# A hybrid gMLP / DeltaNet / cross-attention layer on one core: the triangular inverses' small matmuls in seven bundles instead of four, the first two projection stages cut by pairs of heads, and a planner with other constants

## The chip, the cores and the metric

The kernel runs on one core of one Trainium2 chip, as one launch. The metric is device time in microseconds (us); lower is better.

## The reference

One decoder layer on 1024 tokens of width 2048, all in float32. Cut to what matters here:

```
h = rmsnorm(x); proj = h @ w_in                       # 2048 x 6672
g_u,g_v,g_z, d_q,d_k,d_v,d_z,d_a,d_b, c_q,c_z = split(proj)
out_a = gelu(g_u) * (tril(W_s) layernorm(gelu(g_v)) + b) * silu(g_z)   # per 128-token chunk
q,k,v = silu(causal_conv4([d_q,d_k,d_v]))             # 8 heads of 128
a = strict_lower((k*beta) k^T * decay)                # per head and chunk of tokens
T = inverse(a + I)                                    # unit triangular
o = scan over chunks with T (gated delta rule)        # state 128 x 128 per head
out_b = rmsnorm(o) * silu(d_z)
out_c = softmax(c_q mk^T / sqrt(128)) mv * silu(c_z)  # 256 memory tokens
x = x + concat(out_a, out_b, out_c) @ w_out; y = rmsnorm(x)
```

The kernel uses chunks of 128 tokens, so an inverse is that of a 128 x 128 unit triangular matrix. There are 64 of them: 8 heads, 8 chunks.

## The kernel before

**The big products.** Each float32 product is done as three fp32r matmuls (high x high, high x low, low x high), so each operand is split: a ScalarE copy makes `hi` (`rhi`, `lh`), a VectorE subtraction makes `lo` (`rlo`, `ll`, `lm`). The two halves of the tokens and two halves of the columns form a 2 x 2 block product, done with seven block products instead of eight (`seven`, in the order 2, 1, 6, 5, 3, 7, 4). A *stage* is one such product of seven. Stages one to three have six output tiles of 128 columns in six PSUM banks (`acc` 0 to 3, `dn` 2 and 3); the later ones have four. Stage one is `project_stage(heads_of(0), ...)` (q, k, v of heads 0 to 3), stage two `heads_of(4)`, stage three `zv`, then `C_U`/`C_Z`, `C_CZ`/`C_CQ`, and the output projection, whose last tile is `kd_515`.

**The weights.** For each pair of row blocks `fetch` loads one rectangle for each entry of `columns` into `raw` (two buffers) or `kept` (four): before, one of 512 and one of 256 columns in stages one to three. All these loads are issued by SP.

**The inverses.** `front` makes the decayed matrices of two heads; `inverse` collects 32 matrices, inverts their 32 x 32 diagonal blocks by substitution on VectorE, writes them to DRAM, and `levels` builds the 64 x 64 and 128 x 128 inverses from them with small matmuls on TensorE: 64 of 32 x 32 (`da = gc t`), 96 of 32 x 32 (three products of each of 16 blocks and two halves), and twice 32 of 64 x 64 (`dy`). There are two such batches, `a` during stage two and `b` during stage three. Results go back to DRAM (`ulo`, `umid`, `uhi`, in the trace `uloa`, `umida`, `uhia` for batch `a`), and `load_u` reads them into `ut` for the scan (`scan_step`), whose first matmul of a batch is `dn<-vs,ut`.

**The order.** Nothing is issued where the code stands. `Plan` records every operation, prices it (`price`), lays all of them out several times with a list scheduler that runs forwards (`lay`) and backwards (`late`), keeps the best layout and issues the operations by their planned times. `R.together()` makes a bundle: its matmuls follow each other on TensorE without anything between. `behind(op)` adds a dependence on `op`. Constants of the planner: `SLACK` is added before TensorE may use another engine's result, `DMA_FIXED` is the assumed latency of a transfer, `PASSES` the number of backward passes. Every engine then runs its instructions in that order, and waits where an operand is not there. As all operations are issued by one line of `issue`, the profile gives L398 for all; groups are told apart by tile names.

Of the kernel before, what the change touches and what calls it, by code (L numbers as in the profile page):

```python
# [17 lines left out]
P = 128  # L18
# [44 lines left out]
class Plan:  # L63
    SEEN = {"pe": 55.0, "act": 35.0, "dve": 35.0, "pool": 78.0, "sp": 60.0}
    SLACK = 300.0
    OVERLAP = {"pe": 0.0, "act": 90.0, "dve": 80.0, "pool": 50.0, "sp": 0.0}
    DMA_RATE = 350.0
    DMA_FIXED = 3800.0
    SWITCH = 400.0
    FIRST, SPREAD, PASSES, STRETCH, AHEAD = 0, 1.75, 5, 1.0, 2000.0  # L70
    TABLE, HOLD = 1300.0, 6000.0
# [111 lines left out]
    def price(self, o, name, outs, ins):  # L183
# [218 lines left out]
def kernel(  # L402
# [629 lines left out]
    def levels(gg, tdr, udr, n):  # L1032
# [19 lines left out]
        with rank(1):  # L1052
# [15 lines left out]
            for h in range(2):  # L1068
                turn_in(uhi[low(2 * h), :, low(0)], every(udr[64:96], h))
            with R.together():  # L1070
                for k in range(16):
                    for r in range(4):
                        t = tu[low(r), k] if r % 2 else tlo[low(r), k, low(0)]
                        PE.matmul(da[low(r), k], gc[low(r), k], t, start=True, stop=True)
            S.copy(yc, da)
            with R.together():
                for k in range(16):
                    for h in range(2):
                        r, q = low(2 * h), low(2 * h + 1)
                        PE.matmul(db[q, k], yc[r, k], tu[r, k], start=True, stop=True)  # L1080
                        PE.matmul(db[r, k], yc[q, k], uhi[q, k, low(1)], start=True, stop=True)
                        PE.matmul(da[q, k], tu[r, k], yc[r, k], start=True, stop=True)
            for h in range(2):
                S.copy(tlo[low(2 * h + 1), :, low(0)], da[low(2 * h + 1)])
                V.tensor_copy(uhi[low(2 * h), :, low(1)], db[low(2 * h)])
            S.copy(ux, db)
            sides = [(x_, h, w) for x_ in range(8) for h in range(2) for w in range(2)]
            with R.together():
                for x_, h, w in sides:
# [198 lines left out]

    def seven(left, right, banks, takes, order, rows=False, last=False, first=0):


        for n, key in enumerate(order):
            c, m = divmod(key, 10)
            bank = banks(key)

            def product(t, i, a, ws, part=None, cols=None):
                for u in range(2):
                    l, (hi, lo) = a[u], ws
                    o = bank[t]
                    if rows:  # L1300
                        l = [x_[:, t * P : (t + 1) * P] for x_ in l]
                        r = [x_[:, u * HT : (u + 1) * HT] for x_ in (hi, lo)]
                        if cols:
                            r, o = [x_[:, cols] for x_ in r], o[:, cols]
# [151 lines left out]

    def rights_of(columns):
        return rights_made([
            (lo, width, lambda i, b, j, k=1, at=at, width=width: blk(w_in, NH * i + j, at[b], k, width))
            for lo, (width, at) in zip((0, 2 * HT), columns)  # L1460
        ])

    def ahead(columns, dst):
# [7 lines left out]

        seven(held_left, [rights_of(columns)], lambda m: wide6, {2: take}, (2,))

    def project_stage(columns, done, dest=None, left=h_left, first_yu=None, then=None, made=None, **how):


        n = len(columns)
        banks, yus, yzs = (wide6, yu6, yz6) if n == 2 else (wide, yu, yz)
        yu2 = first_yu or yus
# [28 lines left out]
        if then:  # L1508
            at = 1
            seven(left, rights, lambda m: banks, takes, ORDER[:1], **how)  # L1510
            how.pop("first")
            then()
        seven(left, rights, lambda m: banks, takes, ORDER[1 if made else at:], **how)
# [137 lines left out]
    Q.dma_start(wt, gmlp_ws[0].rearrange("g t s -> t g s"))  # L1651
    tp = dnr.bufs[1]
# [4 lines left out]
    tp = dnr.bufs[1]  # L1657
    for g in range(NG):
        sl = slice(g * P, (g + 1) * P)
        PE.matmul(tp[:, sl], ones, wsT[g], start=True, stop=True)  # L1660
        V.scalar_tensor_tensor(bt[g], tp[:, sl], col2[:, 4 + g : 5 + g], bsb[:, sl], op0=ALU.mult, op1=ALU.add)
    for hf in range(2):
        spatial(hf)
    scan_banks = dnr.bufs[0:2]
    hand = dnr.bufs[3]
    wide = acc
    el = over([abh[:, 0:HT], ring["tn"].bufs.pop()])
    with rank(2.6):
        for hf in range(2):
            for n in range(2):  # L1670
# [104 lines left out]

    def total(r):
        V.scalar_tensor_tensor(r[:, 4:5], r[:, 3:4], 1.0 / D, r[:, 4:5], op0=ALU.mult, op1=ALU.add)

    def close(half_, t):

        r, r0 = ssy[half_][t], half_ * HT + t * P
        total(r)
        rsqrt_to(r[:, 5:6], r[:, 4:5])
# [13 lines left out]

    def square(half_, t, c, cols=slice(0, HT)):
        S.activation(jk[:, cols], ys[half_][t][c][:, cols], AF.Square, accum_out=ssy[half_][t][:, c : c + 1])

# [29 lines left out]
    def out_pair(cp):  # L1830
# [14 lines left out]
        def final(m, key, c, after=None):  # L1845
            put = more(m, key, after)

            def take(t, a, cols=slice(0, HT)):
                r = ssy[key[0]][t]
                if cols.stop - cols.start < HT:  # L1850
                    add(y[key][t][:, cols], a[:, cols], y[key][t][:, cols])
                    square(key[0], t, c, cols)
                    total(r) if cols.start == 0 else close(key[0], t)
                    return
                put(t, a)
                square(key[0], t, c)
                if c == 3:
                    close(key[0], t)
# [60 lines left out]
```

## Time and profile before

| what | value |
|---|---|
| median of 3 runs | 1586.66 us (1584.83 to 1587.31) |
| profiled execution | 1587.73 us |
| its span, first to last instruction | 1586.0 us |
| mean granted TensorE clock | 0.995 |
| busy: PE / PEld / DVE / ACT / POOL | 98% / 83% / 77% / 59% / 6% |
| DMA | 431.40 MB, mean 272 GB/s |

The profile page names the engines PE (TensorE matmul), PEld (its weight loads, beside PE), DVE (VectorE), ACT (ScalarE), POOL (GpSimd) and SP (SyncE, which here issues nearly all DMAs; SPq is its sequencer). Busy time is the union of an engine's instructions; a matmul is shown with its latency, so neighbours overlap, and the time that one costs is the distance to the next start. "Idle before" is an engine's idle time ahead of a group, with what ended it. PEclk is the share of full clock that TensorE was granted.

### The profile page before, as it was taken

The numbers are of one execution on the slowest core, as the hardware profiler recorded it, in microseconds if no ns is written. First come the engines' busy times: TensorE is split into PE (matmuls) and PEld (weight loads), VectorE is DVE, ScalarE is ACT, GpSimd is POOL, SyncE is SP. The second block draws the span as 40 slices with busy tenths as digits, with TensorE's granted clock in tenths as the row PEclk, the third lists the DMA queues.
The fourth block names the chain that finished last, engine by engine and source line by source line (L and its number), as shares of the span: only waits on it lengthen the run. The fifth ranks groups of instructions, "written<-read, shape, count | busy, mean of one in ns | idle before, by whom it ended". The sixth has DMA issues, their size and how long they took to land.

```text
span 1586.0 us, 25201 instructions
## 1 busy us (share of the span) xinstructions
PE 1559.0 (98%) x8773; PEld 1309.6 (83%) x8773; DVE 1219.6 (77%) x1802; ACT 931.7 (59%) x1921; POOL 102.1 (6%) x125
## 2 busy tenths in 40 slices
PE   8999999999999999999999999999999999999997
PEld 7987888888888778888888778888888888888886
DVE  6966844789979756887799667878668888688775
ACT  7832455767854247778864444876657864344455
POOL 0100001010020001110110010000000000000001
PEclk9999999999999999999999999999999999999999
DMA  9999866999988797886989896898868979678657
GB/s 328 305 333 330 288 182 201 323 324 336 301 260 275 236 294 245 263 282 193 276 275 319 240 261 218 279 343 284 257 211 267 310 263 351 214 269 294 227 151 274
DMA packets 338353, 431.40 MB, mean 272 GB/s; under 512 B 77353, under 2 KB 163890, under 8 KB 338226
## 3 DMA queue, kind: packets, MB, share of 16 engines
q1 hardware_dynamic: 336642, 427.09, 84.0%
q0 software_dynamic: 1088, 2.10, 0.4%
q8 instruction: 69, 1.13, 0.3%
q10 hardware_dynamic: 496, 0.61, 0.1%
q14 instruction: 58, 0.48, 0.1%
HBM read 330.29 MB, written 99.42 MB: 271 GB/s over the span
## 4 chain that ended last, share of the span: by engine, by line
PE 85%; DMA 4%; issue 1%; ACT 1%; DVE 1%; SPq 1%; POOLq 0%; POOL 0%; ACTq 0%; DVEq 0%
PE acc L398 53%; PE dn L398 32%; SPq L398 1%; DMA raw<-in_w_in_dram 1%; DMA E<-ed 1%; DMA late<-os 0%; DMA xr<-pd 0%; DMA kd<-late 0%; DMA ut<-uloa 0%; DMA ut<-in_x_dram 0%; DMA qT<-late 0%; DMA ll<-hsd 0%; ACT obs L398 0%; DVE tn L398 0%; ACT rhi L398 0%
## 5 line engine op out<-in xcount | busy, mean ns | idle before, releaser
L398 PE MATMUL acc<-lh,rhi 128*128 128x512 f32 x1024 | 396.6, 396 | 1.8 <-DVE obs L398 1.8
L398 PE MATMUL acc<-lh,rlo 128*128 128x512 f32 x1024 | 387.1, 396 | 0.2 <-DVE rlo L398 0.2
L398 ACT CAST rhi<-raw 128x1024 fp32r<-128x1024 f32 (+1 forms) x148 | 186.6, 1261 | 244.8 <-PE dn L398 119.3
L398 DVE TENSOR_TENSOR rlo<-raw,rhi 128x1024 fp32r<-128x1024 f32 (+1 forms) x148 | 219.3, 1482 | 106.6 <-ACT rhi L398 103.1
L398 PE MATMUL acc<-ll,rhi 128*128 128x512 f32 x688 | 269.9, 397 | 0.0
L398 PEld LDWEIGHTS acc<-lh,rhi 128*128 128x128 f32 x1024 | 193.3, 189 | 39.4 <-DVE obs L398 2.6
L398 PEld LDWEIGHTS acc<-lh,rlo 128*128 128x128 f32 x1024 | 193.0, 189 | 37.5 <-DVE rlo L398 0.7
L398 DVE TENSOR_TENSOR ll<-ll,lh 128x1024 fp32r<-128x1024 f32 x122 | 149.9, 1229 | 17.3 <-ACT lh L398 17.0
L398 PEld LDWEIGHTS acc<-ll,rhi 128*128 128x128 f32 x688 | 129.7, 189 | 24.8 <-DVE ll L398 0.2
L398 ACT CAST lh<-ll 128x1024 fp32r<-128x1024 f32 x122 | 127.9, 1048 | 23.2 <-DMA ll<-hsd 5.6
L398 PE MATMUL acc<-lm,rhi 128*128 128x512 f32 x336 | 133.4, 399 | 0.0
L398 PE MATMUL dn<-lh,rhi 128*128 128x512 f32 x288 | 112.9, 393 | 0.4 <-issue 0.4
L398 PE MATMUL dn<-lh,rlo 128*128 128x512 f32 x288 | 107.6, 393 | 0.0
L398 DVE TENSOR_TENSOR raw<-raw,kept 128x1024 f32<-128x1024 f32 (+1 forms) x56 | 81.1, 1452 | 3.6 <-DMA raw<-in_w_in_dram 3.6
L398 PE MATMUL dn<-ll,rhi 128*128 128x512 f32 x192 | 75.4, 394 | 0.0
L398 PEld LDWEIGHTS acc<-lm,rhi 128*128 128x128 f32 x336 | 63.6, 189 | 12.0
L398 DVE TENSOR_TENSOR rlo<-kept,rhi 128x1024 fp32r<-128x1024 f32 (+1 forms) x29 | 41.9, 1446 | 37.2 <-ACT rhi L398 37.1
L398 ACT CAST rhi<-kept 128x1024 fp32r<-128x1024 f32 (+1 forms) x29 | 35.7, 1230 | 51.4 <-PE dn L398 25.6
L398 POOL TENSOR_TENSOR hs<-hs,mhalf 128x4 f32<-128x4 f32 x32 | 45.8, 1436 | 273.7 <-DVE hs L398 262.6
L398 PEld LDWEIGHTS dn<-lh,rhi 128*128 128x128 f32 x288 | 54.3, 188 | 10.8
L398 PEld LDWEIGHTS dn<-lh,rlo 128*128 128x128 f32 x288 | 53.9, 188 | 10.4
L398 POOL TENSOR_TENSOR small<-small,mhalf 128x1 f32<-128x1 f32 x26 | 21.3, 819 | 580.7 <-DVE small L398 580.7
(412 smaller groups left out, 3395.8 us busy)
## 6 DMA issues: line engine op xcount, KB each, us to landing
raw<-in_w_in_dram SPq DMA_DIRECT2D x120, 512.0 KB
ll<-hsd SPq DMA_DIRECT2D x54, 512.0 KB
raw<-in_w_out_dram SPq DMA_DIRECT2D x48, 512.0 KB
raw<-in_w_in_dram SPq DMA_DIRECT2D x72, 256.0 KB
lm<-hsd SPq DMA_DIRECT2D x26, 512.0 KB
pd<-obs SPq DMA_DIRECT2D x48, 256.0 KB
late<-os SPq DMA_DIRECT2D x44, 256.0 KB
kept<-in_w_in_dram SPq DMA_DIRECT2D x20, 512.0 KB
```

What stands on the lines that cost most here:

```text
L398: o.fn(*o.args, **o.kw)
```

## The change

- `levels`: the first bundle of 64 becomes two of 32, each with its own copy of half the result (`yc`, 128 x 256 instead of 128 x 512). The bundle of 96 becomes three of 32, one product each, the second and third `behind` the one before. The 64 x 64 bundles stay at 32; the first of them is also `behind` the bundle before it. So 4 bundles become 7 in each of the two batches, with the same matmuls.
- `Plan`: `SLACK` 300 to 200, `DMA_FIXED` 3800 to 4200, `PASSES` 5 to 7, and a new `FETCH` of 3500 added to the latency of small matmuls.
- Stages one and two: `heads_of` gives three rectangles of 256 columns (q, k and v of a pair of heads) instead of one of 512 and one of 256; `lay_of` gives each output tile's place in the buffer. The first column half now holds q, k, v of heads 0 and 1 (or 4 and 5).
- The spatial gate's transposes use PSUM bank `dn` 2 instead of `dn` 1, and its two halves are issued each just ahead of that half's scans.
- The last output tile is finished in one piece of 512 columns instead of two of 256.

```diff
@@ class Plan
-    SLACK = 300.0
+    SLACK = 200.0
-    DMA_FIXED = 3800.0
+    DMA_FIXED = 4200.0
-    FIRST, SPREAD, PASSES, STRETCH, AHEAD = 0, 1.75, 5, 1.0, 2000.0
+    FIRST, SPREAD, PASSES, STRETCH, AHEAD = 0, 1.75, 7, 1.0, 2000.0
+    FETCH = 3500.0
@@ price
-            o.lat = 175.0
+            o.lat = 175.0 + (0.0 if out.shape[0] == P or n == P or name == "transpose" else self.FETCH)
@@ levels
+            for e in range(2):
+                ks = slice(8 * e, 8 * e + 8)
+                with behind(R.ops[-1] if e else R.gate), R.together():
+                    for k in range(16)[ks]:
+                        for r in range(4):
+                            t = tu[low(r), k] if r % 2 else tlo[low(r), k, low(0)]
+                            PE.matmul(da[low(r), k], gc[low(r), k], t, start=True, stop=True)
+                S.copy(yc[:, ks], da[:, ks])
+            blocks = [(k, h, low(2 * h), low(2 * h + 1)) for k in range(16) for h in range(2)]
             with R.together():
-                for k in range(16):
-                    for r in range(4):
-                        t = tu[low(r), k] if r % 2 else tlo[low(r), k, low(0)]
-                        PE.matmul(da[low(r), k], gc[low(r), k], t, start=True, stop=True)
-            S.copy(yc, da)
-            with R.together():
-                for k in range(16):
-                    for h in range(2):
-                        r, q = low(2 * h), low(2 * h + 1)
-                        PE.matmul(db[q, k], yc[r, k], tu[r, k], start=True, stop=True)
-                        PE.matmul(db[r, k], yc[q, k], uhi[q, k, low(1)], start=True, stop=True)
-                        PE.matmul(da[q, k], tu[r, k], yc[r, k], start=True, stop=True)
+                for k, h, r, q in blocks:
+                    PE.matmul(da[q, k], tu[r, k], yc[r, k], start=True, stop=True)
             for h in range(2):
                 S.copy(tlo[low(2 * h + 1), :, low(0)], da[low(2 * h + 1)])
+            with behind(R.ops[-1]), R.together():
+                for k, h, r, q in blocks:
+                    PE.matmul(db[r, k], yc[q, k], uhi[q, k, low(1)], start=True, stop=True)
+            for h in range(2):
                 V.tensor_copy(uhi[low(2 * h), :, low(1)], db[low(2 * h)])
+            with behind(R.ops[-1]), R.together():
+                for k, h, r, q in blocks:
+                    PE.matmul(db[q, k], yc[r, k], tu[r, k], start=True, stop=True)
             S.copy(ux, db)
-            with R.together():
+            with behind(R.ops[-1]), R.together():
                 for x_, h, w in sides:
...
@@ seven
-                        at = u * HT + t * P if t < NT else 2 * HT + u * HT // 2 + t % NT * P
+                        at = lay[t][0] + u * lay[t][1]
-                    if last and key == order[-1] and t == NT - 1:
-                        for cols in (slice(0, HT // 2), slice(HT // 2, HT)):
-                            for h in held:
-                                product(t, *h, cols=cols)
-                            takes[key](t, bank[t], cols)
-                        return
@@ project_stage and around
+    def lay_of(columns):
+        los = [sum(2 * w for w, _ in columns[:i]) for i in range(len(columns))]
+        return [(lo + c, w) for lo, (w, _) in zip(los, columns) for c in range(0, w, P)]
-            which, h = (b, h0 + t) if t < NJ else (2, h0 + 2 * b + t - NJ)
+            which, h = t // 2, h0 + 2 * b + t % 2
-        return (HT, (C_Q + c, C_K + c)), (half, (C_DV + c, C_DV + c + half))
+        return tuple((half, (c0 + c, c0 + c + half)) for c0 in (C_Q, C_K, C_DV))
@@ spatial gate
-            bank = dnr.bufs[1]
+            bank = dnr.bufs[2]
-    for hf in range(2):
-        spatial(hf)
-    with rank(2.6):
-        for hf in range(2):
+    for hf in range(2):
+        spatial(hf)
+        with rank(2.6):
             for n in range(2):
                 back_of(2 + n, hf, inv)
```

Three places show what the planner makes of it. The first is TensorE in batch `a`, where the kernel before goes from the bundle of 64 to that of 96. `dn_111` and `dn_112` are the banks of the small products, `gt_434`, `gt_435`, `inv_432`, `inv_433` their operands (`inv_433` holds `yc`); rows on `acc` are matmuls of the running stage.

```order
L398 MATMUL dn_111<-gt_434,inv_432 32x32
L398 MATMUL dn_111<-inv_432 32x32
L398 MATMUL acc_110<-lh,rhi_76 128x512
L398 MATMUL acc_107<-lh,rhi_77 128x512
L398 MATMUL acc_107<-ll,rhi_77 128x512
L398 MATMUL acc_107<-lh,rlo_75 128x512
L398 MATMUL dn_112<-inv_432,inv_433 32x32
L398 MATMUL dn_112<-gt_435,inv_433 32x32
L398 MATMUL dn_111<-inv_433,inv_432 32x32
```

The changed kernel at its third bundle of the same batch:

```order
L399 MATMUL acc_109<-ll,rhi_77 128x512
L399 MATMUL acc_110<-lh,rhi_77 128x512
L399 MATMUL acc_110<-ll,rhi_77 128x512
L399 MATMUL acc_109<-lh,rlo_75 128x512
L399 MATMUL acc_109<-lh,rhi_77 128x512
L399 MATMUL dn_111<-inv_433,inv_432 32x32 x32
L399 MATMUL acc_109<-ll,rhi_77 128x512
L399 MATMUL acc_109<-lh,rlo_75 128x512
L399 MATMUL acc_110<-lh,rlo_75 128x512
L399 MATMUL acc_110<-lh,rhi_77 128x512
```

Before, four matmuls of the stage stand between 64 and 96 small ones; now 18 stand ahead of this bundle of 32 and 19 behind it. Over both batches the gaps are 18 to 25 matmuls; before they were 4, 8 and 4.

The second place is ScalarE in batch `a`. `inv_433<-dn` is the copy of `yc`, `gt_434<-dn` the next copy that batch needs; CAST rows split the stage's operands. Before:

```order
L398 CAST rhi_77<-raw_73 128x1536
L398 CAST lh<-ll 128x1024
L398 COPY inv_433<-dn_111 128x512
L398 COPY inv_433<-dn_112 128x512
L398 COPY gt_434<-dn_111 32x16x32 x2
L398 COPY inv_432<-dn_111 128x512
```

Now:

```order
L399 CAST rhi_77<-raw_73 128x1536
L399 COPY inv_433<-dn_111 128x256
L399 CAST rhi_76<-raw_72 128x1536
L399 COPY inv_433<-dn_111 128x256
L399 CAST lh<-lm 128x1024
L399 COPY gt_434<-dn_111 32x16x32 x2
```

The second half of `yc` now stands behind the cast of a freshly loaded weight tile, `raw_72`.

The third place is SP's queue between batch `a` and the first scan step, which reads `ut_82`. Before:

```order
L398 DMA umida<-gt_434 64x16x64 x2
L398 DMA ut_82<-uloa 32x8x32
L398 DMA ll<-h0d 128x2x512
L398 DMA kept_80<-in_w_in_dram 128x2x512
L398 DMA ut_82<-uhia 64x8x64
L398 DMA kept_80<-in_w_in_dram 128x2x256
L398 DMA raw_72<-in_w_in_dram 128x2x512
L398 DMA ut_82<-umida 64x8x64
```

Now:

```order
L399 DMA ut_82<-uloa 32x8x32
L399 DMA ll<-h0d 128x2x512
L399 DMA ut_83<-uloa 32x8x32
L399 DMA raw_73<-in_w_in_dram 128x2x512
L399 DMA raw_73<-in_w_in_dram 128x2x256
L399 DMA umida<-gt_434 64x16x64 x2
L399 DMA ll<-h0d 128x2x512
L399 DMA ut_82<-umida 64x8x64
```

The last load that the scan step needs, `ut_82<-umida`, now follows its store with one load between instead of six.

More of the change, by code (lines that the diff above doesn't have):

```diff
@@ L1085, in levels @@
+            for h in range(2):
                 V.tensor_copy(uhi[low(2 * h), :, low(1)], db[low(2 * h)])
+            sides = [(x_, h, w) for x_ in range(8) for h in range(2) for w in range(2)]
+            with behind(R.ops[-1]), R.together():
+                for k, h, r, q in blocks:
+                    PE.matmul(db[q, k], yc[r, k], tu[r, k], start=True, stop=True)
             S.copy(ux, db)
-            sides = [(x_, h, w) for x_ in range(8) for h in range(2) for w in range(2)]
-            with R.together():
+            with behind(R.ops[-1]), R.together():
@@ L1287, with seven @@
     ends, chunk_ends = {}, [kvmark[-1]] * 8
-    def seven(left, right, banks, takes, order, rows=False, last=False, first=0):
+    def seven(left, right, banks, takes, order, lay=None, rows=False, last=False, first=0):
         for n, key in enumerate(order):
@@ L1294, in seven, with product @@
             bank = banks(key)
-            def product(t, i, a, ws, part=None, cols=None):
+            def product(t, i, a, ws, part=None):
                 for u in range(2):
@@ L1457, in rights_of @@
     def rights_of(columns):
+        los = [sum(2 * w for w, _ in columns[:i]) for i in range(len(columns))]
         return rights_made([
             (lo, width, lambda i, b, j, k=1, at=at, width=width: blk(w_in, NH * i + j, at[b], k, width))
-            for lo, (width, at) in zip((0, 2 * HT), columns)
+            for lo, (width, at) in zip(los, columns)
         ])
+    def lay_of(columns):
+        los = [sum(2 * w for w, _ in columns[:i]) for i in range(len(columns))]
+        return [(lo + c, w) for lo, (w, _) in zip(los, columns) for c in range(0, w, P)]
     def ahead(columns, dst):
@@ L1470, in take @@
                 Q.dma_start(dst[t], o)
-        seven(held_left, [rights_of(columns)], lambda m: wide6, {2: take}, (2,))
+        seven(held_left, [rights_of(columns)], lambda m: wide6, {2: take}, (2,), lay_of(columns))
     def project_stage(columns, done, dest=None, left=h_left, first_yu=None, then=None, made=None, **how):
         n = len(columns)
-        banks, yus, yzs = (wide6, yu6, yz6) if n == 2 else (wide, yu, yz)
+        lay = lay_of(columns)
+        banks, yus, yzs = (wide6, yu6, yz6) if n > 1 else (wide, yu, yz)
         yu2 = first_yu or yus
@@ L1509, in project_stage @@
             at = 1
-            seven(left, rights, lambda m: banks, takes, ORDER[:1], **how)
+            seven(left, rights, lambda m: banks, takes, ORDER[:1], lay, **how)
             how.pop("first")
             then()
-        seven(left, rights, lambda m: banks, takes, ORDER[1 if made else at:], **how)
+        seven(left, rights, lambda m: banks, takes, ORDER[1 if made else at:], lay, **how)
     def to_heads(h0):
         def done(hf, b, t, y):
-            which, h = (b, h0 + t) if t < NJ else (2, h0 + 2 * b + t - NJ)
+            which, h = t // 2, h0 + 2 * b + t % 2
             Q.dma_start(p_d[which][h][:, hf * HT : (hf + 1) * HT], y)
@@ L1651 @@
     Q.dma_start(wt, gmlp_ws[0].rearrange("g t s -> t g s"))
-    tp = dnr.bufs[1]
+    tp = dnr.bufs[2]
     for g in range(NG):
@@ L1656 @@
         V.tensor_tensor(out=wsT[g], in0=tp[:, g * P : (g + 1) * P], in1=utri, op=ALU.mult)
-    tp = dnr.bufs[1]
+    tp = dnr.bufs[2]
     for g in range(NG):
@@ L1774 @@
     ys = [[[None] * 4 for _ in range(NT)] for _ in range(2)]
-    def total(r):
-        V.scalar_tensor_tensor(r[:, 4:5], r[:, 3:4], 1.0 / D, r[:, 4:5], op0=ALU.mult, op1=ALU.add)
     def close(half_, t):
         r, r0 = ssy[half_][t], half_ * HT + t * P
-        total(r)
+        V.scalar_tensor_tensor(r[:, 4:5], r[:, 3:4], 1.0 / D, r[:, 4:5], op0=ALU.mult, op1=ALU.add)
         rsqrt_to(r[:, 5:6], r[:, 4:5])
@@ L1796, in close, with square @@
             to.dma_start(out[r0 : r0 + P, c * HT : (c + 1) * HT], y)
-    def square(half_, t, c, cols=slice(0, HT)):
-        S.activation(jk[:, cols], ys[half_][t][c][:, cols], AF.Square, accum_out=ssy[half_][t][:, c : c + 1])
+    def square(half_, t, c):
+        S.activation(jk, ys[half_][t][c], AF.Square, accum_out=ssy[half_][t][:, c : c + 1])
     oh = halves(own(os, "oh", "alo1", 4 * HT))
@@ L1846, in final, with take @@
             put = more(m, key, after)
[L1848 to L1854, printed above, removed]
+            def take(t, a):
                 put(t, a)
                 square(key[0], t, c)
+                r = ssy[key[0]][t]
                 if c == 3:
```

2 lines of the change are left out of this document (removed).

## The prediction

> **What bounds the kernel now.** I read the page's first lines, then TensorE's waits, then fine windows around the places with waits, then the chain.
>
> ```profile
> PE 1559.0 (98%) x8773; PEld 1309.6 (83%) x8773; DVE 1219.6 (77%) x1802; ACT 931.7 (59%) x1921; POOL 102.1 (6%) x125
> ...
> q8 instruction: 69, 1.13, 0.3%
> ```
>
> TensorE is busy for 1559.0 of 1586.0 us. No rearrangement takes its matmuls away, so the change can only win what TensorE loses: 27 us of idle time at most, and slow stretches that count as busy. Its waits, with times and the longest:
>
> ```profile
> PE dn L398 <- issue: 5.8, 5, 2.4
> ...
> PE dn L398 <- DMA ut<-uloa: 2.7, 1, 2.7
> PE acc L398 <- DVE obs L398: 1.8, 1, 1.8
> PE dn L398 <- DVE tn L398: 1.7, 1, 1.7
> ...
> PE dn L398 <- DVE kd L398: 0.7, 1, 0.7
> ```
>
> The largest entry waits for nothing that the profile shows. The windows put it at the inverses' bundles (first batch near 552 us, second near 901 us); the first row is a steady stretch for comparison:
>
> ```profile
> core 0: us, PE busy (x), PEclk, DMA share, GB/s
> 280.00:320.00 40.00, 40.00 (x180) 1.00 0.97 326
> 552.77:556.18 3.41, 2.32 (x193) 1.00 0.95 332
> 556.18:559.60 3.42, 3.42 (x10) 0.50 1.06 344
> 576.67:580.08 3.41, 1.19 (x6) 1.00 1.14 279
> 580.08:583.49 3.41, 2.93 (x9) 0.50 1.17 262
> 900.93:904.34 3.41, 1.58 (x121) 1.00 0.92 283
> 904.34:907.75 3.41, 3.41 (x8) 0.50 0.88 259
> ```
>
> Three windows with idle time (1.1, 2.2 and 1.8 us idle of 3.41) are each followed by one of 3.41 us at half clock. A half-clock window does half its work, so it costs 3.41 x 0.5 = 1.7 us, though the second column shows it as busy.
>
> Why would TensorE starve in its own small matmuls? The queue q8 moved 1.13 MB in 69 packets, 16.4 KB each, and 8773 matmuls plus as many weight loads are 17546 instructions, 64 B each: q8 has the size of TensorE's code, fetched in blocks of about 256 instructions. A steady stretch uses 180 x 2 instructions in 40 us, 9 per us; the window at 552.77 uses 193 x 2 in 2.32 busy us, 166 per us. So a bundle of 96 runs through a block in under 2 us. That the stalls are fetches is inferred, not shown.
>
> **The change part by part.** All sums are against the profiled execution, 1587.73 us (span 1586.0 and 1.73 around it), which is 1.07 above the median of 1586.66; the forecast is moved to the median at the end.
>
> *Seven bundles, spread out.* The price of a small matmul and of a switch, from TensorE's timeline at the first bundle of 64, and of an ordinary matmul, from the chain:
>
> ```profile
> 549.80 0.39 PE L398 MATMUL acc<-ll,rhi 128*128 128x512 f32 x1
> 550.02 0.39 PE L398 MATMUL acc<-lh,rlo 128*128 128x512 f32 x1
> 550.34 0.21 PE L398 MATMUL dn<-gt,inv 32*32 32x32 f32 x1
> ...
> 551.44 0.19 PE L398 MATMUL dn<-inv 32*32 32x32 f32 x1
> 551.56 0.73 PE L398 MATMUL acc<-lh,rhi 128*128 128x512 f32 x2
> ...
> 1337.37 65.28 PE acc L398 x288
> ```
>
> An ordinary matmul takes 65.28 / 288 = 0.227 us. From the last one before the bundle to the first behind it are 1.54 us, so 64 small ones cost 1.31: 0.09 to enter, 1.10 for the run, 0.12 to leave. A bundle of 32 then costs about 0.75, and each extra bundle adds 0.2: six of them, +1.2 us (0.6 to 1.8). Against that, 32 small and 18 ordinary matmuls are now 100 instructions in 0.75 + 18 x 0.227 = 4.8 us, 21 per us, an eighth of the density that stalled. I take all 5.8 us of "issue" as gone, and with them the half-clock windows at 556 and 904 us, 2 x 1.7 = 3.4. The Trainium skill, Runtime: NRT & Kernel Launch, section "Instruction fetch mechanics", says that instructions come in blocks of 16 KiB and that the cost of crossing one is mostly hidden. The packet size agrees; a hidden cost would leave the 5.8 us unexplained, and by that rule this term would be nothing (a rival below).
>
> *The copies between bundles.* TensorE runs in order, so a bundle whose operand is late holds up the whole stage. In the first batch the second half of `yc` stands on ScalarE behind the cast of `raw_72`, which waits for a weight load:
>
> ```profile
> L398 ACT CAST rhi<-raw 128x1536 fp32r<-128x1536 f32 x72 | 106.8, 1483 | 131.1 <-PE dn L398 95.4 <-DVE raw L398 8.5 <-DMA sm<-od 8.4
> L398 ACT ACT_TABLE_LOAD x19 | 24.4, 1283 | 2.8 <-issue 2.2 <-DVE small L398 0.3
> L398 ACT COPY inv<-dn 128x512 f32<-128x512 f32 x8 | 4.7, 587 | 21.4 <-PE dn L398 11.9 <-DVE gt L398 4.7 <-issue 4.7
> ...
> 551.96 1.87 SPq L398 DMA_DIRECT2D raw<-in_w_in_dram  x2
> ...
> 119.00 5.78 DMA ut<-in_x_dram
> ...
> 916.38 10.58 DMA raw<-in_w_in_dram
> ```
>
> TensorE reaches its third bundle 2 x 0.75 + 36 x 0.227 = 9.7 us after the first. If SP issues `raw_72` where it does now, 1.6 to 3.5 us after the first bundle (551.96 against 550.34, two issues), a landing takes 5.8 us as in the row at 119, the cast 1.5 and the half copy at most 0.6, the copy is ready 11.4 us after it: a wait of about 2 us. An idle time of 2.2 us brought a half-clock window at 580 us, so this one is at the edge of it; I leave it out. With the 10.58 us of the row at 916 it is 6.5, plus 1.7. I take +2.0 (0 to 8.2). ScalarE also gets 16 more table loads (35 for 19 in the order), 16 x 1.28 = 20.5 us; it is idle for 41% of the span, so nothing, except where one stands ahead of such a copy: 1.3.
>
> *The first scan step.* The wait for `ut` (2.7 us, and the half-clock window at 580) hangs on SP's queue:
>
> ```profile
> 567.68 1.30 SPq L398 DMA_DIRECT2D umida<-gt  x2
> ...
> 573.18 0.61 SPq L398 DMA_DIRECT2D ut<-umida  x1
> ```
>
> Store and load now stand closer (one load between, not six), but the store itself has 19 issues ahead of it since the last bundle. At the 0.65 us that one of the two stores takes, 19 + 4 issues are 15 us, with two landings behind; TensorE gets there 76 matmul times, 17 us, after the last bundle. It will be late again. I take no change (from -4.4, both gone, to +3).
>
> *Spatial gate's bank and order of the second scans.* TensorE's work there is the same and hidden in the stage; the wait for `obs` at a stage's start (1.8) had a weight load of 10.58 us behind it that shares the queues with batch `b`. I take half of it as gone, -0.9 (-1.8 to 0).
>
> *Column blocks by pairs.* 56 more loads on SP, with rows of 1 KB for 2 KB:
>
> ```profile
> 555.88 2.46 SPq L398 DMA_DIRECT2D kept<-in_w_in_dram  x3
> ...
> SPq L398 <- PE dn L398: 222.8, 129, 7.8
> ```
>
> 56 x 0.82 = 46 us of SP's time, which lies in the 222.8 us that SP waits for TensorE alone. Where SP is the limit, in the start (TensorE's wait for `tn`, 1.7 us, ends a chain through SP and the load of `x` at 119), seven of them stand ahead of the last `x` load: at most 7 x 0.82 = +5.7, at best -1.7, as that load is the 130th on SP now and was the 132nd. I take 0. That conv and `qk` of the first pair could start earlier moves VectorE's and ScalarE's work, not TensorE's.
>
> *The last tile.* Two halves cost a wait, the 0.7 us for `kd`:
>
> ```profile
> 1573.84 0.28 PE L398 MATMUL dn<-oh 128*128 128x256 f32 x1
> ...
> 1577.59 0.28 PE L398 MATMUL dn<-rhi,fl 128*128 128x256 f32 x1
> ...
> 1574.04 0.69 DVE L398 TENSOR_TENSOR kd<-dn,kd 128x512 f32<-128x512 f32 x1 [0.72 <-PE dn L398]
> ...
> 1577.91 0.42 DVE L398 TENSOR_TENSOR kd<-dn,kd 128x256 f32<-128x256 f32 x1
> ...
> 1574.83 0.63 ACT L398 ACTIVATE jk<-kd 128x512 bf16<-128x512 f32 x1
> ...
> 1578.72 0.42 ACT L398 ACTIVATE jk<-kd 128x256 bf16<-128x256 f32 x1 [0.53 <-DVE kd L398]
> ```
>
> Whole, 12 matmuls of 0.227 from 1573.84 start last at 1576.34, 1.25 earlier than 1577.59, and last 0.1 longer; the final add and square are 0.27 and 0.21 longer. Net -0.7 at best; as the add now stands behind the scaling of the tile before, I take -0.5 (-0.7 to +0.6).
>
> *Less slack for TensorE.* Results may be planned 0.1 us closer to their use. All its waits outside the places above are under 3 us, so I take +1.0 (0 to 3).
>
> Sum: -5.8 - 3.4 + 1.2 + 2.0 - 0.9 - 0.5 + 1.0 = -6.4 us. That is 1587.73 - 6.4 = 1581.3 for a profiled execution, 1580.3 on the scale of the median.
>
> **The rivals.**
>
> *Late operands at the bundles (slower).* Each batch now hands over between TensorE and a copy six times where it did three, at fixed places in the stage. If in both batches one copy waits behind a cast whose weight load takes 10.58 us, each costs 6.5 + 1.7 = 8.2: -6.4 - 2.0 + 16.4 = +8, 1594.7. It is a loss from 11.6 us of such waits on. For it: ScalarE's order above, a DMA share of 0.9 to 1.1 in those windows, less slack. Against: TensorE has 4 us of other work between bundles and waited for no copy at all in the kernel before. Chance 0.18.
>
> *The stalls are not fetches (it doesn't do what it says).* Small matmuls then starve for another reason, in 14 bundles as in 8, and the half-clock windows stay too. The sum is +1.2 + 2.0 - 0.9 - 0.5 + 1.0 = +2.8, 1589.5. For it: the profile names no releaser. Against: the density. Chance 0.06. The rule of the Trainium skill quoted above would give this case.
>
> *SP pays at the start.* With +5.7 there, the sum is -0.7: 1586.0. For it: the chain through SP at 119. Against: the `x` load moved ahead by two places. Chance 0.10.
>
> *The scan's wait goes too.* -6.4 - 4.4 = -10.8, 1575.9; with the other good ends -17, 1569.5. It belongs to the faster side.
>
> **How the numbers follow.** What a measurement can tell from no change is 0.2%, 3.2 us: below 1583.5 is faster, above 1589.8 slower. The forecast with its better cases has 0.66, and nearly all of that lies below 1583.5. The start's rival and half of the fetch rival end within 0.2%, with 0.02 of the forecast's own upper end: 0.15 in all. The late copies and what is left make 0.19. The range reaches from 1571 (short of the sum of all best ends) to 1590 (the fetch rival inside, the slower one outside).
>
> **What would show it.** Right: no "issue" entry above 1 us in TensorE's waits; PEclk 1.00 at 550 to 570 and 895 to 925; the entry `ut<-uloa` or its neighbour still there with 1 to 5 us; a last matmul some 1.2 us earlier against the end of the tile before it. Wrong: "issue" at the bundles, which would refute the density; or new entries for ACT `inv` or `gt`, or DMA `raw`, of more than 2 us there, which is the slower rival; or `tn` above 4 us in the first 160 us.

## The result, and the profile after

| | before | after |
|---|---|---|
| median | 1586.93 us (1584.83 to 1587.31, 4 runs) | 1575.95 us (1574.93 to 1577.73, 4 runs) |
| ratio to before | | 0.9934, 95% interval 0.9919 to 0.9949 |
| profiled execution | 1587.73 us, span 1586.0 | 1575.38 us, span 1573.7 |
| mean granted clock | 0.995 | 0.999 |

The change is faster by 11.0 us, inside the range; the forecast was 6.4. Half of this document is about what those 11 us are made of, because the last runs showed that they are not all owed to the change.

The page's lines for the kernel after: the busy times and the packets.

```profile
PE 1556.9 (99%) x8761; PEld 1307.3 (83%) x8761; DVE 1220.2 (78%) x1800; ACT 954.9 (61%) x1937; POOL 98.2 (6%) x125
...
DMA packets 353585, 431.40 MB, mean 274 GB/s; under 512 B 78249, under 2 KB 193458, under 8 KB 353458
```

TensorE is busy for 2 us less, though more bundles lengthen its work; the half-clock windows of the kernel before count as busy time. The pair blocks bring 15,000 more packets (338,353 before) for the same bytes. TensorE's waits of the kernel after, complete (total, times, longest):

```profile
PE dn L399 <- DMA y<-in_mem_norm_g_dram: 3.0, 1, 3.0
PE dn L399 <- ACT inv L399: 1.6, 1, 1.6
PE dn L399 <- DMA kept<-in_mem_dram: 1.2, 1, 1.2
PE dn L399 <- ACT rhi L399: 1.0, 1, 1.0
PE dn L399 <- ACT vs L399: 0.5, 2, 0.2
PE acc L399 <- ACT xr L399: 0.3, 1, 0.3
PE dn L399 <- DVE states L399: 0.2, 1, 0.2
```

"Issue" (5.8), `ut` (2.7), `obs` (1.8), `tn` (1.7) and `kd` (0.7) are gone; the entries for `y`, `kept` and `rhi` belong to the first 10 us and are as before. One new entry is large, 1.6 us for `inv`, the copy between two bundles; the other small ones (`vs`, `xr`, `states`) come to 1.0 us, where the kernel before had 0.8 (`os`, `rlo`, `vs`). Three stretches of both kernels, TensorE alone (width, busy, matmul records, clock, DMA share, GB/s): the end of stage one, batch `a`, batch `b`. Before:

```profile
340.00:500.00 160.00, 160.00 (x778) 1.00 0.93 301
500.00:620.00 120.00, 115.57 (x959) 0.97 0.85 256
880.00:960.00 80.00, 73.91 (x748) 0.98 0.84 235
```

After:

```profile
340.00:500.00 160.00, 160.00 (x776) 1.00 0.95 304
500.00:620.00 120.00, 118.16 (x965) 1.00 0.77 238
880.00:960.00 80.00, 80.00 (x791) 1.00 0.89 246
```

Width less busy is the idle time: 4.4 + 6.1 = 10.5 us at the two batches before, 1.8 after, and no half-clock window after. These three rows are the yardstick for the experiments.

### The profile page after: what moved, and what is told of

Same layout as the page of the kernel before. It is cut to its first block, busy times and chain, and to the rows that moved or that the text cites. A ratio compares the mean times of both kernels' runs of the same rounds, so it can differ in the third digit from the quotient of the medians.

```text
span 1573.7 us, 25225 instructions
## 1 busy us (share of the span) xinstructions
PE 1556.9 (99%) x8761; PEld 1307.3 (83%) x8761; DVE 1220.2 (78%) x1800; ACT 954.9 (61%) x1937; POOL 98.2 (6%) x125
## 4 chain that ended last, share of the span: by engine, by line
PE 96%; DVE 1%; issue 1%; DMA 1%; ACT 0%; SPq 0%; POOLq 0%; POOL 0%; ACTq 0%
PE acc L399 59%; PE dn L399 37%; DMA raw<-in_w_in_dram 0%; DMA kept<-in_mem_dram 0%; DVE os L399 0%; DVE states L399 0%; DVE rlo L399 0%; ACT vs L399 0%; DVE obs L399 0%; DVE raw L399 0%; ACT jk L399 0%; DVE ll L399 0%; DVE steps L399 0%; SPq L399 0%; ACT obs L399 0%
## 5 line engine op out<-in xcount | busy, mean ns | idle before, releaser
L399 PE MATMUL acc<-lh,rhi 128*128 128x512 f32 x1024 | 389.7, 395 | 0.0
L399 PE MATMUL acc<-lh,rlo 128*128 128x512 f32 x1024 | 380.0, 394 | 0.1
L399 POOL TENSOR_TENSOR small<-small,mhalf 128x1 f32<-128x1 f32 x26 | 16.3, 630 | 681.7 <-DVE small L399 681.7
L399 DVE TENSOR_TENSOR lm<-lm,lh 128x1024 fp32r<-128x1024 f32 x42 | 51.2, 1219 | 7.4 <-ACT lh L399 7.3
L399 PE MATMUL acc<-rlo,lh 128*128 128x512 f32 x144 | 56.3, 391 | 0.0
```

Of the source, the lines that this page charges most:

```text
L399: o.fn(*o.args, **o.kw)
```

## The experiments

Twelve kernels ran. Ratios are to the kernel before on the same chip. The last three columns come from rows like those above: idle time in 500 to 620 and 880 to 960 us together, half-clock windows of 3.41 us in there, idle time in 340 to 500 us. They come from one profiled execution each, and executions of one kernel scatter: the kernel before, run 27 times beside e1 to e4, lay between 1581.3 and 1592.1 us, so differences of an us or two between rows mean little.

| kernel | blocks | bundles | constants | median us | ratio, 95% | idle at batches | half clock | idle 340–500 |
|---|---|---|---|---|---|---|---|---|
| before | old | 4 | old | 1586.93 | 1 | 10.5 | 3 | 0 |
| e1 | old | 7 | old | 1585.16 | 0.9983 (0.9969–0.9997) | 4.4 | 2 | 0 |
| e7 | pairs | 4 | old | 1592.16 | 1.0019 (1.0008–1.0031) | 12.3 | 5 | 0 |
| e2 | old | 4 | new | 1587.31 | 1.0006 (0.9995–1.0016) | 6.1 | 1 | 1.1 |
| e11 | pairs | 7 | new, `FETCH` 0 | 1595.43 | 1.0059 (1.0046–1.0071) | 5.1 | 4 | 0 |
| **after** | pairs | 7 | new | 1575.95 | 0.9934 (0.9919–0.9949) | 1.8 | 0 | 0 |
| e6 | pairs | 4 | new | 1576.82 | 0.9922 (0.9910–0.9934) | 3.3 | 0 | 0 |
| e10 | pairs | 7 | new, `DMA_FIXED` 4300 | 1581.48 | 0.9970 (0.9959–0.9980) | 0.6 | 0 | 1.1 |
| e5 | old | 7 | new | 1586.81 | 0.9998 (0.9986–1.0010) | 3.2 | 0 | 3.5 |
| e9 | pairs | 7 | new, `SLACK` 210 | 1588.00 | 1.0008 (0.9999–1.0016) | 0.8 | 0 | 3.2 |
| e12 | pairs, old bank | 7 | new | 1588.01 | 1.0014 (1.0005–1.0023) | 3.0 | 0 | 4.4 |
| e3 | old | 7 | new | 1591.34 | 1.0038 (1.0024–1.0051) | 2.6 | 0 | 7.4 |

e1, e2, e3 and e7 are the kernel before with parts of the change; e5, e6, e9 to e12 the changed kernel with parts undone.

**What starves the bundles: e4 and e8.** Both add 192 matmuls of 32 x 32, on constants that are always there, to stage one of the kernel before; nobody reads their results. e4 has them in one block, e8 in six bundles with 36 stage matmuls between. The edit (e4, the matmul's operands shortened; in e8 `22 <= len(chunk_ends) < 28` and `range(32)`):

```diff
                     chunk_ends.append(R.ops[-1])
+                    if len(chunk_ends) == 22:
+                        with rank(-1), behind(R.ops[-1]), R.together():
+                            for z in range(192):
+                                zr = slice(z % 4 * 32, z % 4 * 32 + 32)
+                                PE.matmul(dnr.bufs[1][zr, ...], ident[zr, zr], ident[zr, zr], ...)
```

> The kernel before with 192 additional 32x32 matmuls on resident constants in one block in stage one, near 240 us, far from the batches; they wait for nothing and nobody reads them. Theory (instruction fetch): 384 instructions in about 3.3 us, so an 'issue' wait of 1 to 4 us in or just behind the block, and a half-clock window after it; 4 to 9 us more in all. Rival (the stalls at the batches were waits on operands that the profile does not name): no 'issue' wait there, 3.3 us more.

> The kernel before with the same 192 additional 32x32 matmuls as in the dense block, in six bundles of 32 with 36 stage matmuls between them. Theory (instruction fetch): no 'issue' wait and PEclk 1.00 from 190 to 245 us; about 6 x 0.75 = 4.5 us more there. Rival (small matmuls starve TensorE wherever they stand): waits and half-clock windows near each bundle, 8 us or more.

One execution each: 1600.90 us for e4, 1595.22 for e8 (the kernel before on the same chip, in the median: 1586.11 and 1588.18). e4, TensorE's waits between 195 and 225 us, and then its windows at the block:

```profile
PE dn L398 <- issue: 7.8, 2, 4.5
```

```profile
200.24:203.66 3.42, 1.97 (x195) 1.00 0.91 277
203.66:207.07 3.41, 0.40 (x46) 1.00 0.77 210
207.07:210.48 3.41, 1.35 (x104) 0.50 0.34 112
210.48:213.90 3.42, 2.13 (x66) 0.50 0.02 5
213.90:217.31 3.41, 3.41 (x10) 0.50 0.63 172
```

e8, the stretch that holds all six bundles:

```profile
190.00:250.00 60.00, 60.00 (x628) 1.00 0.63 175
```

The same matmuls stall for 7.8 us in one block and for nothing in six. No operand can be late there, so it is their density. (The second stall lies in windows with a DMA share of 0.34 and 0.02, so it is not a crowd on the queues either; the first lies at 0.91 and 0.77.) What was expected of e8 came true in this stretch; of e4 the kind came true and the size was too small: 7.8 us of stalls for 1 to 4, three half-clock windows for one, and 14.8 us in all for 4 to 9. Both also stall longer than the kernel before at the old bundles of the two batches, 8.6 us in e4 and 11.3 in e8 where it has 5.8. So the length of these stalls is no fixed price of a bundle.

The records say more. The stretch from one "issue" stall to the next, in the kernel before at batch `b`, in e4 at its block and in e8 at batch `a`:

```profile
902.74:908.94 6.20, 5.05 (x128) 0.72 0.85 267
908.94:913.00 4.06, 3.36 (x127) 1.00 0.65 189
```

```profile
206.66:211.76 5.10, 1.75 (x128) 0.54 0.30 99
```

```profile
568.49:574.41 5.92, 2.50 (x128) 0.50 1.07 364
```

These neighbouring stalls (twelve such pairs in seven kernels) are 127 or 128 matmul records apart, with as many weight loads some 256 instructions. That is the block of the prediction, 16.4 KB or one packet of q8 at 64 B an instruction: TensorE stops each time where a block of its code ends. The traces also hold every packet of q8, 16,384 bytes each, with its times. Beside TensorE's stalls (us from the span's start):

| kernel | q8 packet, from and to | TensorE goes on at | after a stall of | packet's end to going on |
|---|---|---|---|---|
| before | 900.32 to 901.29 | 902.76 | 2.40 | 1.47 |
| before | 906.59 to 907.57 | 908.95 | 1.15 | 1.38 |
| e4 | 203.86 to 205.23 | 206.67 | 4.46 | 1.44 |
| e4 | 209.38 to 210.33 | 211.77 | 3.35 | 1.44 |
| e8 | 572.08 to 573.09 | 574.42 | 3.42 | 1.33 |

The kernels together have 31 stalls called "issue". 28 of them end 1.1 to 1.5 us after a packet of q8 has landed, though these packets come only every 23 us in the mean. So these stalls are code fetches, which the prediction could only infer. The other three (e1 0.5 us, e2 1.4, e8 0.2) stand ahead of the first scan step's `dn<-vs,ut`, 5 to 13 us after the last such packet; what they wait for is not shown. The Trainium skill, Runtime: NRT & Kernel Launch, section "Instruction fetch mechanics", has the same block of 256 instructions and calls the crossing mostly hidden: that holds in e8's stretch (nothing at six bundles) and fails at e4's block (4.5 and 3.3 us at two crossings).

**One part at a time: e1, e2, e7.** e1 is the kernel before with the change's `levels`:

```diff
+            for e in range(2):
+                ks = slice(8 * e, 8 * e + 8)
+                with behind(R.ops[-1] if e else R.gate), R.together():
...
+            with behind(R.ops[-1]), R.together():
+                for k, h, r, q in blocks:
```

> The kernel before with the seven smaller bundles alone; the planner keeps its old constants, so the bundles stand 3 to 7 stage matmuls apart (in the changed kernel 18 to 25). Theory (TensorE starves for instructions where small matmuls stand densely): the density hardly falls, so 'issue' waits of 4 to 7 us and at least two half-clock windows remain; 1584 to 1590 us. Rival (the size of a bundle is what counts): 'issue' under 1 us, 1577 to 1580 us.

Its bundles stand 3 to 7 stage matmuls apart, as nothing tells the planner to spread them. "Issue" falls from 5.8 to 2.2 us (1.7 of it fetches), less than the 4 to 7 that were expected, and two half-clock windows stay:

```profile
PE dn L398 <- issue: 2.2, 3, 1.1
...
PE dn L398 <- ACT inv L398: 1.5, 1, 1.5
```

e2 is the kernel before with the four constants, and so with distance but with the old bundles:

```diff
-    SLACK = 300.0
+    SLACK = 200.0
-    DMA_FIXED = 3800.0
+    DMA_FIXED = 4200.0
-    FIRST, SPREAD, PASSES, STRETCH, AHEAD = 0, 1.75, 5, 1.0, 2000.0
+    FIRST, SPREAD, PASSES, STRETCH, AHEAD = 0, 1.75, 7, 1.0, 2000.0
+    FETCH = 3500.0
```

> The kernel before with the planner's new constants alone (SLACK, DMA_FIXED, PASSES, FETCH); four bundles of 64, 96, 32 and 32, now 19 to 28 stage matmuls apart. Theory (density): the bundle of 96 still runs through 192 instructions in under 2 us, so 0 to 2 us of 'issue' per batch, and the rest of the stalls goes; 1577 to 1583 us. Rival (bundle size): 'issue' stays at 4 to 6 us, 1584 us or more.

```profile
PE acc L399 <- issue: 3.6, 1, 3.6
...
PE dn L399 <- issue: 1.8, 2, 1.4
```

Still 5.4 us of it (4.0 of it fetches), and no gain, as the rival had it. e7 is the kernel before with the pair blocks:

```diff
-        return (HT, (C_Q + c, C_K + c)), (half, (C_DV + c, C_DV + c + half))
+        return tuple((half, (c0 + c, c0 + c + half)) for c0 in (C_Q, C_K, C_DV))
```

> The kernel before with the column blocks by pairs alone: old bundles, constants, spatial gate and last tile. Theory (TensorE had no waits in stage one before, so earlier fronts give nothing): 'issue' stays at 4 to 7 us, 1584 to 1589 us. Rival (the blocks bring a gain of their own): 1576 to 1582 us.

It is slower than either expectation, with 8.6 us of "issue". So no part alone was measured to give more than 0.2%.

**Two parts, or the change less one: e3, e5, e6.** e3 has e1's and e2's edits together; e5 is the changed kernel with the old blocks (e7's edit turned round); e6 is the changed kernel with the four old bundles.

> The kernel before with bundles and constants together, and nothing of the column blocks, the spatial gate's bank or the last tile. Theory (the gain is the batches' stalls, half-clock windows and the wait for ut, and all of it comes from these two edits): no 'issue' entry, PEclk 1.00 at both batches, 1575 to 1579 us. Rival (the pairs of heads bring a large part): 1581 to 1585 us.

> The changed kernel with the old column blocks (512 and 256) in stages one and two. Theory (with blocks by pairs, q, k and v of a pair are there after the second of seven products, so the fronts' work is not crowded at the stage's end): TensorE waits of 5 to 12 us in stage one between 370 and 420 us, as with bundles and constants alone; 1583 to 1592 us. Rival (those waits were an accident of one layout, the blocks carry nothing): no more than 3 us of waits there, 1574 to 1579 us.

> The changed kernel with the four old bundles (64, 96, 32, 32), still 19 to 27 stage matmuls apart. Theory (a bundle of 96 alone outruns the instruction fetch): 'issue' waits of 3 to 6 us and one or two half-clock windows; 1580 to 1585 us. Rival (the planner's distance between bundles is enough): 1575 to 1578 us.

e3 and e5 have no "issue" entry and no half clock at the batches, and yet gain nothing; e3 is slower than either expectation. Their loss has moved. TensorE's waits of e3 between 340 and 440 us, ahead of the first inverses:

```profile
PE dn L399 <- DVE ai L399: 2.0, 1, 2.0
PE dn L399 <- DVE inv L399: 1.7, 1, 1.7
PE acc L399 <- DVE ll L399: 1.3, 1, 1.3
```

That stretch has no such wait before or after. In e5 the waits there come to 3.5 us, between its two expectations. e6 is as fast as the changed kernel: with the planner's distance and the pair blocks the bundles' size bought nothing that can be measured. It has one fetch stall of 0.8 us; e2, with the same four bundles, the same constants and the old blocks, has 4.0.

At this point the pair blocks looked decisive: with the new constants, 1575.95 us with them against 1586.81 without, and 1576.82 against 1587.31 with the old bundles. A mechanism was at hand too: the work on two heads' q, k and v is spread out instead of crowding at 380 to 420 us. The last four runs were made to test that against mere luck of the layout.

**Edits that mean nothing: e9 and e10.** The changed kernel with one constant moved by a hair:

```diff
-    SLACK = 200.0
+    SLACK = 210.0
```

```diff
-    DMA_FIXED = 4200.0
+    DMA_FIXED = 4300.0
```

> The changed kernel with SLACK 210 in place of 200: an edit that means nothing by itself but makes the planner lay everything out anew. Theory A (pair blocks together with the new constants really leave less to wait for): 1575 to 1579 us, no issue entry above 1 us, no window at half clock, and no more than 2 us of new waits. Theory B (the changed kernel is one lucky layout among many that scatter by some 10 us): anywhere from 1576 to 1592 us, and if it is above 1582, with waits at a place where the changed kernel has none.

> The changed kernel with DMA_FIXED 4300 in place of 4200: a second edit without a meaning of its own. Theory A: 1575 to 1579 us, waits for transfers as in the changed kernel. Theory B: between 1576 and 1592 us, and not near the run with SLACK 210.

1588.00 and 1581.48 us: theory A fell, and theory B, one good layout among many that scatter, stands. Ten units of `SLACK` remake TensorE's order (of its 8,761 matmul records, 3,644 have the same tiles and shape at the same place in both traces) and cost 12 us. The three stretches of e9:

```profile
340.00:500.00 160.00, 156.82 (x752) 0.99 0.93 294
500.00:620.00 120.00, 119.25 (x953) 1.00 0.82 253
880.00:960.00 80.00, 80.00 (x786) 1.00 0.88 239
```

The batches are as good as in the changed kernel, better by 1.1 us; 3.2 us and a half-clock window are lost in the first stretch, pair blocks or not. Its two longest waits there are 1.1 us for `rhi` and 1.0 for `lhs`.

**The two other parts: e11 and e12.** The changed kernel with `FETCH` at 0, and with the spatial gate as before:

```diff
-    FETCH = 3500.0
+    FETCH = 0.0
```

```diff
-            bank = dnr.bufs[2]
+            bank = dnr.bufs[1]
...
+    for hf in range(2):
+        spatial(hf)
...
-        spatial(hf)
```

> The changed kernel with FETCH at 0, so that the seven bundles are planned 3 to 8 stage matmuls apart and not 36; everything else stays. If the distance is what removes the stalls: issue entries of 2 to 8 us at the bundles, one to three windows at half clock, 1580 to 1587 us. If the pair blocks and the other constants are enough: no issue entry above 1 us, 1575 to 1579 us. From bundles alone in the kernel before, which stand at the same distance, I have 2.2 us of issue and one such pair of windows, so I lean to some 1580 us.

> The changed kernel with the spatial gate's transposes back on bank 1 and both its halves ahead of the second scans. If the bank matters as the prediction had it (half of a wait of 1.8 us for obs): 1576 to 1578 us, a wait for obs of 1 to 2 us at a stage's start between 920 and 1010 us. If it does not: 1574.5 to 1577.5 us and no such wait. Theory B would have it anywhere between 1576 and 1592 us.

The bundles of the changed kernel lie 18 to 25 stage matmuls apart, not 36 as the expectation of e11 says. e11, at 1595.43 us, is the slowest of the twelve but for e4, and slower than either expectation: "issue" is back with 2.5 us, and four half-clock windows with it. It also has waits that have nothing to do with code (2.4 for a load of the spatial gate, 2.3 for `obs`), so its 19.5 us are not the price of `FETCH`. e12 lies at 1588.01 without any wait for `obs`; its loss is again ahead of the first inverses, in waits for `os`, `jk` and `lhs` (1.5, 1.5 and 1.3 us). It also has a fetch stall of 0.7 us at a bundle, with the seven bundles and `FETCH` at 3500.

What the bank is worth can't be read from this: the edit laid out the whole kernel anew.

**What follows.** Two things separate in the table. At the batches the effect repeats. The six kernels with seven bundles and `FETCH` at 3500 (after, e3, e5, e9, e10, e12) have 0.6 to 3.2 us idle there and no half-clock window, and e6 with 3.3 us is close; of fetch stalls the six have 0.7 us in all, in e12. The kernel before, e1, e2, e7 and e11 have 4.4 to 12.3 us and one to five windows, and 1.7 to 8.6 us of fetch stalls. Against the kernel before, the six gain 7.3 to 9.9 us of idle time and 5.1 us of half clock, and pay 2.0 us for more bundles (worked out below for the changed kernel): by this estimate 10 to 13 us in each layout. Elsewhere nothing repeats. The same six lose 0 to 7.4 us in the first stretch alone, and lie anywhere from 1576 to 1591 us, 1585.3 in the mean: the new layouts give back 0 to 15 us, and the changed kernel is the fastest of its neighbours. The three kernels with the old constants have no idle time in the first stretch, and of the nine with the new ones six have some, which speaks for a price of the smaller `SLACK` or of its companions; which of them was not tried alone. What the pair blocks and the gate's bank are worth by themselves stays open, since each edit remakes the layout. No kernel beat the changed one; e6 is its equal.

## Why the prediction was right, and where it was not

The profiled executions differ by 12.3 us. By the prediction's own terms:

*Issue stalls, -5.8: right, and the cause now shown.* Each small float32 matmul stands in the trace as two, 64 rows for a bundle of 32, and by the blocks of 128 rows these are instructions. The prediction counted rows for the density that stalled (166 instructions per us) and matmuls for the new one (21); counted alike it is (64 + 18) x 2 / 4.8 = 34 per us. e8 does not test that: its bundles lie 9.1 us apart, (64 + 36) x 2 / 9.1 = 22 per us. The changed kernel itself shows that 34 can do, with no stall, and e12 that it is not far from the edge, with one of 0.7 us at that distance. Nor is one half of the change the means: seven bundles without the distance keep 1.7 us of fetch stalls (e1), the distance with four bundles 4.0 and 0.8 (e2, e6), and only both together have next to none in each layout tried.

*Half-clock windows, -3.4: the two at the bundles went, and the third with them,* because the wait for `ut` went: -5.1.

*Six extra bundles, +1.2: mis-sized.* From the chain of waits of the kernel after (start, us, what; the busy time is a little under the time that TensorE loses):

```profile
548.03 0.68 PE dn L399 x50
548.72 1.14 PE acc L399 x4
...
559.65 1.20 PE dn L399 x64
```

and of e6, a bundle of 96 that met no stall:

```profile
920.37 2.16 PE dn L399 x148
922.53 1.37 PE acc L399 x5
```

By start to next start, a bundle of 32 with `gt` costs 0.77 us, as forecast; one from the old bundle of 96 costs 1.22. So one of 64 became 2 x 0.77 for 1.31, but one of 96 became 3 x 1.22 = 3.66 for 2.26. Both batches: 2 x (0.23 + 1.40) = +3.3 against bundles that don't stall, +2.0 against those of before as they ran. The step that failed priced all six like the first kind.

*The copy behind the cast, +2.0: right to 0.4 us, and by that chain.* ScalarE and TensorE after (start, us, operation, idle time before):

```profile
548.80 0.37 ACT L399 COPY inv<-dn 128x256 f32<-128x256 f32 x1 [2.36 <-issue]
557.85 1.47 ACT L399 CAST rhi<-raw 128x1536 fp32r<-128x1536 f32 x1 [8.67 <-DMA raw<-in_w_in_dram]
559.23 0.37 ACT L399 COPY inv<-dn 128x256 f32<-128x256 f32 x1
```

```profile
551.61 6.08 DMA raw<-in_w_in_dram
```

The second copy stands behind the cast, the cast behind a landing of 6.08 us (5.78 in the prediction), and the copy is done 11.6 us after the first bundle (11.4). TensorE waited 1.6 us. The prediction put the wait at the edge of a half-clock window and left it out; the wait fell across two windows and none followed.

*The first scan step, 0: wrong; it was worth -2.7 and a half-clock window.* "It will be late again" was the step that failed. SP and TensorE after:

```profile
590.03 3.82 SPq L399 DMA_DIRECT2D umida<-gt  x2
...
597.44 1.28 SPq L399 DMA_DIRECT2D ut<-umida  x2
...
602.09 0.60 PE L399 MATMUL dn<-vs,ut 128*128 128x128 f32 x4
```

The last bundle starts at 583.63, so the loads are issued 15.1 us after it: the 15 us of the prediction. But it put two landings behind those 15, and the store's landing lies within them, in the 3.6 us between the end of the stores and the loads. Only the load's own landing is left, and TensorE comes 3.4 us after the last load's issue and 18.5 after the bundle, not 17.

*`obs`, -0.9, and `tn` in the start (column blocks, 0): both waits went whole, -1.8 and -1.7.* Neither can be put down to the parts that the prediction tied them to: the idle time of the first 160 us is 5.3 to 5.5 us in after, e2, e5, e7 and e9, and 6.2 to 7.0 in before, e1, e3, e6, e10, e11 and e12, with old and pair blocks in both lots. That is the layout.

*The last tile, -0.5: right.* The last matmul starts 2.49 us after the tile's first, where it was 3.75:

```profile
1562.11 0.39 PE L399 MATMUL dn<-oh 128*128 128x512 f32 x1
...
1564.60 0.39 PE L399 MATMUL dn<-rhi,fl 128*128 128x512 f32 x1
```

From its first matmul to the end of the span were 1586.02 - 1573.84 = 12.18 us and are 1573.66 - 1562.11 = 11.55: -0.6.

*Less slack, +1.0: +0.2 in this layout* (1.0 us of other waits for 0.8), but the neighbours lose 1 to 7 us in the first stretch. If that belongs to this term, its upper end of 3 was too low; no run shows that it does.

The sum as measured: -5.8 - 5.1 + 2.0 + 1.6 - 2.7 - 1.8 - 1.7 - 0.6 + 0.2 = -13.9. The 1.6 us between that and -12.3 I can't place.

Of the rivals, late copies came once, with 1.6 us, and not with 8.2. "Not fetches" is refuted by the 128 records and the packets of q8. SP paid nothing at the start. The one that came was "the scan's wait goes too", 1575.9 us, to 0.1 us; but a layout whose neighbours lie at 1581 and 1588 makes that agreement an accident. What the prediction lacked is a term for the layout itself: it summed the places that it could see, and took every other place to stay as it was, while the planner remade them all.

## What to carry to other kernels

When a planner lays out the whole program, compare a change not with one kernel before but with a few layouts of the same change, made by edits that mean nothing: here these alone moved the time by 5.5 and 12 us, as much as the change's 11. Judge a part by the stretch that it is meant to mend (idle time and clock there, in every layout), and the whole by the spread. Small matmuls without other work between them can outrun the loading of their own code: look for waits without a releaser, count the records from one to the next, and see whether a packet of the instruction queue has landed just before each ends.

## What the hardware showed that was not expected

**Half clock without an idle window.** Window of the wait and the next one, e9 and then e10:

```profile
416.32:419.73 3.41, 1.33 (x11) 1.00 1.02 350
419.73:423.14 3.41, 3.41 (x11) 0.50 1.15 201
```

```profile
1135.42:1138.83 3.41, 1.90 (x7) 1.00 1.02 356
1138.83:1142.24 3.41, 3.41 (x10) 0.50 0.94 290
```

and the kernel after at its third bundle:

```profile
555.49:558.91 3.42, 2.52 (x12) 1.00 1.02 368
558.91:562.32 3.41, 2.67 (x71) 1.00 1.09 383
```

The windows lie on a fixed grid of 3.41 us. e10 lost 1.5 us in one of them, and the next ran at half clock; the changed kernel lost 0.9 and 0.7 us in two neighbours, and nothing followed. So a wait of some 1.5 us can cost 1.7 us more or nothing more. How it is spread over the windows is not the whole rule: in e5 two neighbouring windows were less busy than e10's and kept the full clock, as did the next.

```profile
414.24:417.65 3.41, 1.87 (x13) 1.00 1.03 354
417.65:421.07 3.42, 1.68 (x9) 1.00 0.96 301
421.07:424.48 3.41, 3.41 (x19) 1.00 0.91 176
```

Small matmuls don't settle it either: 2.32 busy us with 193 records were followed by half clock in the kernel before, 2.36 us with 120 records in e8 (908.98 to 912.40) were not. What decides stays open. The Trainium skill, TensorE: Matmul & The Clock Gate, section "What's actually happening", has the same window and gives half rate after one or more idle windows; here it followed windows that were busy for up to 2.4 of their 3.41 us (e4, 572.30 to 575.71: 2.37). In e4 three windows in a row ran at half clock, 10.24 us.
